# Another order of up and down steps in two Strassen MLPs, and a buffer of its own for one of their weight quads

## The chip, the cores and the metric

The kernel runs on one core of one Trainium2 chip. The metric is the device time of one execution in microseconds, the median of several runs. Before the change it is 1105.84 us (three runs, 1102.9 to 1106.29).

## The reference

A decoder trunk of two layers over 512 tokens of width 1024, in float32. Layer 0 mixes with multi-head latent attention (8 heads, low-rank queries and keys, a rotary part), layer 1 with sliding-window attention (16 query heads over 4 key heads, window 128, a bias by relative position, a sink per head). Each mixer and each MLP is followed by a layer norm of the residual:

```python
# every layer
x = LN(alpha * x + mixer(x))
x = LN(alpha * x + mlp(x))          # alpha = sqrt(2), LN with gain g and bias b

def _mlp(x, w_up, w_down):          # w_up: 1024 x 4096, w_down: 4096 x 1024
    h = jax.nn.relu(x @ w_up)
    return (h * h) @ w_down
```

The output is x after the second layer, 512 x 1024.

## The kernel before, in words

**Arithmetic.** A float32 operand is split into a high part in the matmul format fp32r and a low part, the rest. A product is three matmuls: high by high, high by low, low by high (`three`, `group`; the matmuls are all recorded at L86). A split (L76 to L79) is a copy on ScalarE (ACT, L78) and a subtraction on VectorE (DVE) or GpSimd (POOL), L79. The high part's name ends in h, the low part's in l: `wh`, `wl` are weights, `xth`, `xtl` factors made of x. `fac` holds both parts of a factor of a down step.

**The MLP.** The 4096 hidden columns are four blocks, q = 0 to 3. Each product of a block with x is done by Winograd's form of Strassen's scheme: seven products of half-size matrices in place of eight. So a block has seven up steps, U1 to U7, and, for the first three blocks, seven down steps, D1 to D7; the last block's down product is done plainly, in eight chunks named "down". An up step is 48 matmuls of 256 columns, a down step 24 of 512.

A step multiplies a sum of quarters of x (or of the hidden block) by a sum of quarters of the weights. The hidden block's four quarters are `a11`, `a12`, `a21`, `a22`. They come out of PSUM by sums on DVE as soon as the products they need are done: a12 after U2, a11 after U6, a21 after U7, a22 after U4. Each then goes through a relu and a square on ACT (L622, L623). D1's factor is a11, D2's is a12, and D5, D3, D7, D6 and D4 take sums or single quarters that need a21 and a22.

**Weights.** `queue_seven` makes the sums of weight quarters by memory traffic: quad "a" is loaded by SP for product 1, and after each use a DMA issued by POOL adds another quarter to it in place (L144), for products 5, 6 and 4 in turn. Quad "b" does the same for products 3 and 7; product 2 has a raw tile. Each quad has two halves (jp = 0, 1). The sum for a step can be added only once the split for the step before in that chain has read the quad, and the next split waits until the added quarter has landed. U's quad "b" and D's quad "b" share a tile (`quadb`).

Each step needs two halves of split weights, and there are four buffers for them, so a step's split begins when the step two places back has freed its buffers. A list, `stream`, holds the loads and splits in the order of the steps, and `weights()` keeps it a few entries ahead of the matmuls.

**What sets the order.** Three strings (L41, L42) give the order of steps: `FIRST_STEPS` is the start, `STEPS` the pattern repeated for blocks 0 and 1, `LAST_STEPS` for block 2 with the end; a prime means the next block. TensorE's matmuls are pinned to program order by `pe()`, a call of `keep_in_program_order`. On the other engines a scheduler places the instructions; before the change the loads issued by SP are placed by it too. A dictionary `at` (L668 to L672) says behind which step the code for a down step's factor stands.

**The start of an MLP.** `layer_norm` closes the mixer token tile by token tile, its last operations on POOL (L327, L328), with the gain and bias in a tile `gb` (`load_gb`, L308 and L309). `XFactors.turn` transposes a token tile of x on TensorE (L533), copies it out of PSUM (`xf`, L536), and after the fourth tile makes the sums 5, 3, 6, 7, 4 of x's quarters (L498 to L506) and splits them. Steps U1 and U2 need only the first two tiles; U5 comes next.

**Attention.** The weights of the heads (`w_h`) and of the output projection (`w_o`) are loaded by SP through two `raw` buffers (L115). Beside them SP writes and rereads a table of position biases through DRAM (`ed`, L904, `band`, L907).

Of the kernel before, what the change touches and what calls it, by code (L numbers as in the profile page):

```python
# [8 lines left out]
F32 = mybir.dt.float32  # L9
# [6 lines left out]
P = 128  # L16
D = 1024
# [7 lines left out]
NFF = 4  # L25
# [12 lines left out]

ON_POOL = ("w_h", "w_o", "w_sq", "w_so")

STEPS = "U7 D1 D2 U4 U'1 D5 U'2 D3 U'5 D6 D7 U'3 D4 U'6"  # L41
FIRST_STEPS, LAST_STEPS = "U'1 U'2 U'5 U'3 U'6", "U7 D1 D2 U4 U'1 D5 U'2 D3 U'5 D6 D7 U'3 U'6 U'7 U'4 D4"  # L42

AHEAD_S, AHEAD_B = 3, 2

# [5 lines left out]
def build(tc, nc, io, out):  # L51
    with ExitStack() as top:
# [10 lines left out]
        def nm(s):  # L63
            n_names[0] += 1
            return f"{s}_{n_names[0]}"

        def bank(cols=512, tag="mm", bufs=6):
            return ps.tile([P, cols], F32, tag=tag, bufs=bufs, name=nm(tag), padded_shape=[P, 512])

        def tbank():  # L70
            return bank(512, "tr", 2)

        def f32(ap):
            return ap.bitcast(F32)

        def split(dst_h, dst_l, src, engine=None):  # L76

            nc.scalar.activation(dst_h, src, AF.Copy)  # L78
            (engine or nc.vector).tensor_sub(dst_l, src, f32(dst_h))  # L79

        def pe(ins):
            tc.keep_in_program_order(ins)
# [13 lines left out]
        def tiles_of_weights():  # L96
            wh = wp.tile([P, 1024], F32R, tag="wh", bufs=4, name=nm("wh"))
            wl = wp.tile([P, 1024], F32R, tag="wl", bufs=4, name=nm("wl"))
            return wh, wl

        def raw_tile():
            return wp.tile([P, 1024], F32, tag="raw", bufs=2, name=nm("raw"))

        def queue(name, ap, low=nc.vector):


            def make(pieces=1, between=None):
                cols = ap.shape[-1]
                raw = raw_tile()
                wh, wl = tiles_of_weights()  # L110
                for j in range(pieces):
                    c = slice(j * cols // pieces, (j + 1) * cols // pieces)
                    if between:
                        between(j)
                    nc.sync.dma_start(raw[:, c], ap[:, c])  # L115
                    split(wh[:, c], wl[:, c], raw[:, c], low)
                return wh, wl

            stream.append((name, make))
# [3 lines left out]
        def queue_seven(name, key, chunk):  # L123

            quads = {}

            def half(a, jp):
                if a not in quads:  # L130
                    if (key, a) == ("U", "a"):
                        quads[a] = xp.tile([P, 4, 512], F32, tag="xt", bufs=8, name=nm("wq"))
                    else:
                        quads[a] = mlp_pool[0].tile([P, 4, 512], F32, tag="quad" + a, bufs=1, name=nm("wq"))
                return quads[a][:, 2 * jp : 2 * jp + 2, :]

            def flat(ap):
                return ap.rearrange("p a b -> p (a b)")

            def grown(a, jp, *more):  # L140
                wh, wl = tiles_of_weights()
                split(wh, wl, flat(half(a, jp)))
                if more:
                    nc.gpsimd.dma_start(half(a, jp), chunk(*more, jp), accum_op=ALU.add)  # L144
                return wh, wl

            def loaded(a, jp, at, *more):
                nc.sync.dma_start(half(a, jp), chunk(*at, jp))
                return grown(a, jp, *more)

            def alone(jp):
                raw = raw_tile()
                nc.sync.dma_start(raw.rearrange("p (a b) -> p a b", a=2), chunk(1, 0, jp))
                wh, wl = tiles_of_weights()
                split(wh, wl, raw)
                return wh, wl

            of = {
                1: lambda jp: loaded("a", jp, (0, 0), 0, 1),
                5: lambda jp: grown("a", jp, 1, 1),  # L160
                6: lambda jp: grown("a", jp, 1, 0),
                4: lambda jp: grown("a", jp),
                2: alone,
                3: lambda jp: loaded("b", jp, (1, 1), 0, 1),
                7: lambda jp: grown("b", jp),
            }
# [79 lines left out]
        class Feat:  # L246
# [11 lines left out]
            def turn(self, t):  # L258
                turn_tokens(t, self)
# [4 lines left out]
        b = bank()  # L264
# [28 lines left out]
        half = cp.tile([P, 1], F32, name="half")  # L293
# [10 lines left out]
        xs = [None] * NT  # L304

        def load_gb(g, b):
            gb = xtok.tile([P, 2, D], F32, tag="gb", bufs=1, name=nm("gb"))
            nc.sync.dma_start(gb[:, 0, :], g.partition_broadcast(P))  # L308
            nc.sync.dma_start(gb[:, 1, :], b.partition_broadcast(P))  # L309
            return gb  # L310

        def layer_norm(t, gb, dst):
# [197 lines left out]
        class XFactors(Factors):  # L510
# [14 lines left out]
            def turn(self, t):  # L525
                half_, tk = t // 2, slice(t % 2 * P, (t % 2 + 1) * P)
                if t % 2 == 0:
                    self.xf[half_] = self.mp.tile([P, 2, 4, 256], F32R, tag="fac", bufs=3, name=nm("xf"))
                for n in range(2):
                    pt = tbank().rearrange("p (a b) -> p a b", a=4)  # L530
                    for a in range(4):
                        k = n * 4 + a
                        pe(nc.tensor.transpose(pt[:, a, :], xs[t][:, k * P : (k + 1) * P], ident))  # L533
                    if half_ == 0:
                        split(self.part(n + 1, 0)[:, :, tk], self.part(n + 1, 1)[:, :, tk], pt)
                    nc.scalar.activation(f32(self.xf[half_][:, n, :, tk]), pt, AF.Copy)  # L536
                if t == NT - 1:
                    quarters = [f32(self.xf[i][:, n]) for i in range(2) for n in range(2)]
                    for n in (5, 3, 6, 7, 4):
                        split(self.part(n, 0), self.part(n, 1), self.sum(n, *quarters))  # L540

        def mlp(src, gb, dst, mp):
# [123 lines left out]
            steps = list(steps_of())  # L666

            at = {}  # L668
            for i, (which, q, n) in enumerate(steps):
                if which == "D":  # L670
                    needs = {1: 6, 2: 2, 4: 4}.get(n, 4)
                    i_q = steps.index(("U", q, needs))  # L672
                    i_last = steps.index(("U", q + 1, 6)) - 1 if q == NFF - 2 and n in (4, 7) else i
                    at.setdefault(max(min(i - 2, i_last), i_q), []).append((q, n))
            for i, (which, q, n) in enumerate(steps):
                if which == "U":
# [11 lines left out]
                for q_, n_ in sorted(at.get(i, ()), key=lambda x: [y[2] for y in steps if y[0] == "D" and y[1] == x[0]].index(x[1])):  # L688
                    blocks[q_].factor(n_)

            b = blocks[NFF - 1]
            b.factor(2)
            b.factor(1)
# [19 lines left out]
        with tc.tile_pool(name="mla", bufs=1) as mp:  # L713
# [64 lines left out]
            for kp in range(4):  # L778
                wh, wl = weights("w_kv")
                for t in range(NT):  # L780
                    tk = slice(t * P, (t + 1) * P)
                    for kk in range(2):
                        k, c = 2 * kp + kk, slice(kk * 320, (kk + 1) * 320)
# [19 lines left out]
            for t in range(NT):  # L803
# [194 lines left out]
        xtok = top.enter_context(tc.tile_pool(name="xtok", bufs=1))  # L998

        for t in range(NT):  # L1000
            xs[t] = xtok.tile([P, D], F32, tag="x", bufs=NT, name=nm("x"))
            nc.sync.dma_start(xs[t], io["x"][t * P : (t + 1) * P, :])
        gb = load_gb(io["ln_mix_g"][0], io["ln_mix_b"][0])
        x2 = Feat()
        with tc.tile_pool(name="mlp0", bufs=1) as mp:
            mlp_pool[0] = mp
            x1 = XFactors(mp)
            proj.finish(gb, x1)
            gb = load_gb(io["ln_mlp_g"][0], io["ln_mlp_b"][0])
            mlp(x1, gb, x2, mp)  # L1010


        with tc.tile_pool(name="swa", bufs=1) as mp:
# [56 lines left out]
            pts = [None] * SQH  # L1070
# [103 lines left out]
            run_steps([(h, 0) for h in range(SQH)], AHEAD_B, scores, turn, mix, fill, 1, 1)  # L1174

        gb = load_gb(io["ln_mix_g"][1], io["ln_mix_b"][1])
        with tc.tile_pool(name="mlp1", bufs=1) as mp:
            mlp_pool[0] = mp
            x3 = XFactors(mp)
            proj.finish(gb, x3)  # L1180
            gb = load_gb(io["ln_mlp_g"][1], io["ln_mlp_b"][1])
            mlp(x3, gb, None, mp)


# [107 lines left out]
```

## Time and profile before

| | us |
|---|---|
| median of three runs | 1105.84 |
| profiled execution, its own time | 1104.43 |
| its span, first to last instruction | 1102.7 |
| TensorE (PE) busy in it | 1026.0 (93%) |
| VectorE busy | 785.3 (71%) |
| ScalarE busy | 562.9 (51%) |
| GpSimd busy | 248.6 (23%) |
| mean granted TensorE clock | 0.971 |

The page gives one profiled execution. A row of the timeline has the start, the duration, the engine, the line and the operation with output and inputs; in brackets stands how long the engine was idle before it, and whose result ended that. The waits are the same brackets summed by what ended them: total, times, longest. The granted clock is a share of TensorE's full rate. Up steps begin at 201 us of the span in layer 0 and at 733 us in layer 1.

### The profile page before, as it was taken

How to read it: one execution, taken by the hardware profiler on the slowest of the kernel's cores; microseconds unless marked ns; L12 is line 12 of the kernel's file. 1: busy time of each engine (PE TensorE's matmuls, PEld its weight loads, DVE VectorE, ACT ScalarE, POOL GpSimd, SP SyncE). 2: the span in 40 equal slices, each digit the busy share in tenths (PEclk: the TensorE clock that was granted, in tenths of full speed). 3: DMA queues.
4: the chain of work that ended last, by engine and by line, in shares of the span. 5: the costliest groups of instructions: out<-in, count | busy, mean ns of one | idle time of the engine just before them, and what ended most of it. 6: DMA issues, size and time to landing. Idle time of an engine off the chain costs nothing.

```text
span 1102.7 us, 15934 instructions
## 1 busy us (share of the span) xinstructions
PE 1026.0 (93%) x6148; PEld 909.2 (82%) x6148; DVE 785.3 (71%) x1257; ACT 562.9 (51%) x861; POOL 248.6 (23%) x218
## 2 busy tenths in 40 slices
PE   8999998898998998999999998998899899899996
PEld 7878886797887887888889887887788788788885
DVE  4688855885866856877586788587586686677755
ACT  4456632645634734736156687345473564455530
POOL 0121001511220310320134564043022022112104
PEclk9999998988999998999999999998899999899999
DMA  6241224684884886783242322438568668867432
GB/s 206 89 150 58 91 103 170 129 170 108 180 202 131 176 190 159 150 170 101 85 133 88 96 78 67 147 79 160 143 149 180 175 155 177 203 153 153 81 111 76
DMA packets 60823, 149.55 MB, mean 136 GB/s; under 512 B 5275, under 2 KB 10572, under 8 KB 60748
## 3 DMA queue, kind: packets, MB, share of 16 engines
q0 software_dynamic: 24320, 58.73, 30.3%
q1 hardware_dynamic: 35852, 89.23, 23.7%
q8 instruction: 48, 0.79, 0.3%
q10 hardware_dynamic: 576, 0.59, 0.2%
q14 instruction: 27, 0.22, 0.1%
HBM read 146.41 MB, written 4.22 MB: 137 GB/s over the span
## 4 chain that ended last, share of the span: by engine, by line
PE 48%; issue 19%; DVE 13%; ACT 8%; DMA 7%; POOL 3%; SPq 0%; POOLq 0%; ACTq 0%; DVEq 0%
PE mm L86 43%; DVE wl L79 6%; DMA wq<-in_up 5%; ACT wh L78 4%; PE tr L86 3%; POOL rs L300 1%; ACT a L622 1%; ACT a L623 1%; DVE fac L79 1%; POOL x L328 1%; POOL x L327 1%; DMA xraw<-in_xT 1%; DVE ptl L79 1%; DVE xtl L79 1%; ACT fac L78 1%
## 5 line engine op out<-in xcount | busy, mean ns | idle before, releaser
L86 PE MATMUL mm<-wh,fac 128*128 128x512 f32 (+1 forms) x944 | 305.8, 401 | 28.4 <-ACT fac L78 24.4
L78 ACT ACTIVATE wh<-wq 128x1024 fp32r<-128x1024 f32 x168 | 175.2, 1057 | 247.0 <-DMA wq<-in_up 107.4
L86 PE MATMUL mm<-xth,wh 128*128 128x256 f32 (+1 forms) x1000 | 266.2, 292 | 13.3 <-ACT xth L78 6.1
L79 DVE TENSOR_TENSOR wl<-wq,wh 128x1024 fp32r<-128x1024 f32 x168 | 207.1, 1244 | 90.0 <-ACT wh L78 88.8
L86 PE MATMUL mm<-xth,wl 128*128 128x256 f32 (+1 forms) x872 | 255.2, 293 | 3.0 <-DVE wl L79 3.0
L86 PEld LDWEIGHTS mm<-wh,fac 128*128 128x128 f32 x944 | 181.5, 195 | 74.4 <-ACT fac L78 27.0
L86 PE MATMUL mm<-xtl,wh 128*128 128x256 f32 (+1 forms) x744 | 219.1, 295 | 2.2 <-DVE xtl L79 2.2
L86 PEld LDWEIGHTS mm<-xth,wh 128*128 128x128 f32 x1000 | 184.8, 194 | 18.9 <-ACT xth L78 6.9
L86 PE MATMUL mm<-wl,fac 128*128 128x512 f32 (+1 forms) x472 | 187.8, 398 | 0.0
L86 PEld LDWEIGHTS mm<-xth,wl 128*128 128x128 f32 x872 | 169.0, 194 | 6.3 <-DVE wl L79 4.0
L86 PEld LDWEIGHTS mm<-xtl,wh 128*128 128x128 f32 x744 | 144.5, 194 | 5.5 <-DVE xtl L79 3.0
L78 ACT ACTIVATE wh<-raw 128x1024 fp32r<-128x1024 f32 (+4 forms) x93 | 92.0, 992 | 110.7 <-PE mm L86 58.8
L144 POOL DMA_DIRECT2D wq<-in_up x64 | 77.4, 1211 | 299.6 <-DVE wl L79 290.6
L79 DVE TENSOR_TENSOR wl<-raw,wh 128x1024 fp32r<-128x1024 f32 (+4 forms) x74 | 88.9, 1205 | 50.0 <-ACT wh L78 50.0
L86 PEld LDWEIGHTS mm<-wl,fac 128*128 128x128 f32 x472 | 92.2, 195 | 18.0
L144 POOL DMA_DIRECT2D wq<-in_down x48 | 42.4, 884 | 159.9 <-DVE wl L79 155.9
L300 POOL TENSOR_TENSOR rs<-v,half 128x1 f32<-128x1 f32 x24 | 24.5, 1022 | 238.9 <-DVE v L319 200.9
L79 POOL TENSOR_TENSOR wl<-raw,wh 128x1024 fp32r<-128x1024 f32 (+1 forms) x19 | 40.1, 2115 | 82.9 <-ACT wh L78 78.5
L86 PE MATMUL mm<-wh,oh 128*128 128x512 f32 x128 | 51.9, 405 | 3.0 <-ACT wh L78 3.0
L86 PE MATMUL mm<-wl,oh 128*128 128x512 f32 x128 | 51.0, 399 | 0.5 <-DVE wl L79 0.5
L86 PE MATMUL mm<-wh,ol 128*128 128x512 f32 x128 | 50.9, 398 | 0.0
L454 DVE TENSOR_TENSOR x<-mm,x 128x512 f32<-128x512 f32 (+1 forms) x49 | 32.9, 675 | 21.4 <-PE mm L86 21.0
(196 smaller groups left out, 1795.8 us busy)
## 6 DMA issues: line engine op xcount, KB each, us to landing
wq<-in_up POOLq DMA_DIRECT2D x64, 512.0 KB, 7.8
wq<-in_down POOLq DMA_DIRECT2D x48, 512.0 KB, 8.1
wq<-in_up SPq DMA_DIRECT2D x32, 512.0 KB, 6.1
raw<-in_down SPq DMA_DIRECT2D x28, 512.0 KB, 4.6
wq<-in_down SPq DMA_DIRECT2D x24, 512.0 KB, 6.2
raw<-in_up SPq DMA_DIRECT2D x16, 512.0 KB, 4.7
raw<-in_w_o SPq DMA_DIRECT2D x8, 512.0 KB, 3.3
raw<-in_w_sq SPq DMA_DIRECT2D x8, 512.0 KB, 3.3
```

The source lines that it names most:

```text
L78: nc.scalar.activation(dst_h, src, AF.Copy)
L79: (engine or nc.vector).tensor_sub(dst_l, src, f32(dst_h))
L86: pe(nc.tensor.matmul(dst, st, mv, start=first and i == 0, stop=last and i == len(pairs) - 1, **kw))
L144: nc.gpsimd.dma_start(half(a, jp), chunk(*more, jp), accum_op=ALU.add)
L300: nc.gpsimd.tensor_tensor(r, v, half, ALU.pow)
L327: nc.gpsimd.tensor_mul(x[:, b], x[:, b], gb[:, 0, b])
L328: nc.gpsimd.tensor_add(x[:, b], x[:, b], gb[:, 1, b])
L454: nc.vector.tensor_add(xs[t][:, c], b, xs[t][:, c])
L622: nc.scalar.activation(self.g[done], self.g[done], AF.Relu)
L623: nc.scalar.activation(self.g[done], self.g[done], AF.Square)
```

## The change

Four edits.

1. In the step order, U4 stands behind U7 and ahead of D1 and D2, where it stood behind D2. So U6 and U4 have one step between them in place of three. The rule that places the factors' code is written anew for it.
2. U's quad "b" lies in the tile of the layer norm's gain and bias (`gb`), no longer in the tile that D's quad "b" uses. The norm that follows the MLP therefore loads its gain and bias late, behind the last U7; the load for the norm ahead of the MLP stays where it is, and U's quad "b" follows its last reader.
3. The first sum of x's quarters, for U5, is made per token tile, with the PSUM bank of the transposition as one operand.
4. All loads issued by SP are pinned to program order.

```diff
-STEPS = "U7 D1 D2 U4 U'1 D5 U'2 D3 U'5 D6 D7 U'3 D4 U'6"
-FIRST_STEPS, LAST_STEPS = "U'1 U'2 U'5 U'3 U'6", "U7 D1 D2 U4 U'1 D5 U'2 D3 U'5 D6 D7 U'3 U'6 U'7 U'4 D4"
+STEPS = "U'1 D5 U'2 D3 U'5 D6 D7 U'3 D4 U'6 U'7 U'4 D'1 D'2"
+FIRST_STEPS, LAST_STEPS = "U'1 U'2 U'5 U'3 U'6 U'7 U'4 D'1 D'2", "U'1 D5 U'2 D3 U'5 D6 D7 U'3 U'6 U'7 U'4 D4"
...
-                    nc.sync.dma_start(raw[:, c], ap[:, c])
+                    pe(nc.sync.dma_start(raw[:, c], ap[:, c]))
...
                     if (key, a) == ("U", "a"):
                         quads[a] = xp.tile([P, 4, 512], F32, tag="xt", bufs=8, name=nm("wq"))
+                    elif (key, a) == ("U", "b"):
+                        quads[a] = xtok.tile([P, 4, 512], F32, tag="gb", bufs=1, name=nm("wq"))
...
-                nc.sync.dma_start(half(a, jp), chunk(*at, jp))
+                pe(nc.sync.dma_start(half(a, jp), chunk(*at, jp)))
...
+                pts = []
                 for n in range(2):
                     pt = tbank().rearrange("p (a b) -> p a b", a=4)
+                    pts.append(pt)
...
                     nc.scalar.activation(f32(self.xf[half_][:, n, :, tk]), pt, AF.Copy)
+                if half_ == 1:
+                    if t % 2 == 0:
+                        self.a = self.scratch()
+                    nc.vector.tensor_sub(self.a[:, :, tk], pts[0], f32(self.xf[1][:, 1, :, tk]))
+                    split(self.part(5, 0)[:, :, tk], self.part(5, 1)[:, :, tk], self.a[:, :, tk])
                 if t == NT - 1:
                     quarters = [f32(self.xf[i][:, n]) for i in range(2) for n in range(2)]
-                    for n in (5, 3, 6, 7, 4):
+                    for n in (3, 6, 7, 4):
...
-                    needs = {1: 6, 2: 2, 4: 4}.get(n, 4)
-                    i_q = steps.index(("U", q, needs))
-                    i_last = steps.index(("U", q + 1, 6)) - 1 if q == NFF - 2 and n in (4, 7) else i
+                    i_q = steps.index(("U", q, {1: 6, 2: 2}.get(n, 4)))
+                    i_last = steps.index(("U", q + 1, {2: 2, 3: 2}.get(n, 6))) - 1
                     at.setdefault(max(min(i - 2, i_last), i_q), []).append((q, n))
...
+            gb = gb()
             b = blocks[NFF - 1]
             b.factor(2)
...
-            gb = load_gb(io["ln_mlp_g"][0], io["ln_mlp_b"][0])
-            mlp(x1, gb, x2, mp)
+            mlp(x1, lambda: load_gb(io["ln_mlp_g"][0], io["ln_mlp_b"][0]), x2, mp)
```

The same `pe()` stands around the loads of x, of `gb` and of product 2's raw tile, and the same `lambda` at the second MLP.

**Where instructions move: ScalarE between U6 and D1 of the first block.** The first list is the order before; `wq_409` is U's quad "a", `wq_487` is D's quad "a", the raw tiles are D2's weights, L622 and L623 are the relu and the square, `fac_494` is D1's factor.

```order
L78 ACTIVATE wh_488_2430<-wq_487_2428 128x1024
L78 ACTIVATE wh_495_2499<-wq_487_2428 128x1024
L78 ACTIVATE wh_498_2506<-raw_497_2504 128x1024
L622 ACTIVATE a11_492_2463<-a11_492_2463 128x1024
L78 ACTIVATE wh_505_2570<-raw_504_2568 128x1024
L623 ACTIVATE a11_492_2463<-a11_492_2463 128x1024
L622 ACTIVATE a21_501_2535<-a21_501_2535 128x1024
L78 ACTIVATE fac_494_2495<-a11_492_2463 128x1024
L78 ACTIVATE fac_503_2565<-a12_463_2243 128x1024
L623 ACTIVATE a21_501_2535<-a21_501_2535 128x1024
L78 ACTIVATE wh_507_2574<-wq_409_1910 128x1024
L78 ACTIVATE wh_511_2606<-wq_409_1910 128x1024
```

And the order of the change, where `wq_494` is D's quad "a" and `fac_500` is D1's factor:

```order
L78 ACTIVATE wh_486_2428<-wq_409_1910 128x1024
L78 ACTIVATE wh_492_2492<-wq_409_1910 128x1024
L78 ACTIVATE wh_495_2498<-wq_494_2496 128x1024
L631 ACTIVATE a11_490_2460<-a11_490_2460 128x1024
L78 ACTIVATE wh_501_2562<-wq_494_2496 128x1024
L632 ACTIVATE a11_490_2460<-a11_490_2460 128x1024
L631 ACTIVATE a21_498_2528<-a21_498_2528 128x1024
L78 ACTIVATE fac_500_2558<-a11_490_2460 128x1024
L78 ACTIVATE fac_507_2626<-a12_465_2246 128x1024
L78 ACTIVATE wh_504_2569<-raw_503_2567 128x1024
```

The two copies of U4's weights moved from behind D1's and D2's factors to the place ahead of a11's relu, and D1's and D2's weights each moved one step back; the row of relu, square and factor is as it was. On TensorE U4's 48 matmuls moved ahead of D1's in the same way.

**ScalarE at the start of the MLP.** The order before, from U3's first weight copy on (`wq_460` is U's quad "b", `xth_466` the high part of U5's and U3's factors, `xf` the copied transposes, L605 and L607 the a12 quarter):

```order
L78 ACTIVATE wh_461_2214<-wq_460_2212 128x1024
L605 ACTIVATE a12_463_2243<-mm_452_2141 128x512
L78 ACTIVATE wh_473_2305<-wq_460_2212 128x1024
L605 ACTIVATE a12_463_2243<-mm_454_2168 128x512
L536 ACTIVATE xf_455_2194<-tr_464_2271 128x4x128
L536 ACTIVATE xf_455_2194<-tr_465_2277 128x4x128
L607 ACTIVATE a12_463_2243<-a12_463_2243 128x1024
L78 ACTIVATE xth_466_2283<-uv_468_2285 128x1024
```

The order of the change (`wq_462` is U's quad "b", `xth_458` the factors' high part):

```order
L78 ACTIVATE xth_458_2206<-uv_457_2204 128x4x128
L614 ACTIVATE a12_465_2246<-mm_453_2165 128x512
L540 ACTIVATE xf_454_2191<-tr_466_2274 128x4x128
L616 ACTIVATE a12_465_2246<-a12_465_2246 128x1024
L540 ACTIVATE xf_454_2191<-tr_467_2280 128x4x128
L78 ACTIVATE wh_463_2217<-wq_462_2215 128x1024
L78 ACTIVATE xth_458_2206<-uv_457_2204 128x4x128
L78 ACTIVATE wh_472_2305<-wq_462_2215 128x1024
```

U5's factor is now copied in two halves, the first earlier than its whole was. U3's first weight copy stands between the last `xf` copy and the second half, where it stood ahead of the last tile's copies.

**SP in the attention blocks.** The order before, with the two transfers of the bias table at L904 and L907:

```order
L115 DMA raw_141_715<-in_w_uv 128x1024
L115 DMA raw_159_770<-in_w_h 128x640
L115 DMA raw_186_870<-in_w_h 128x640
L904 DMA ed_148<-p_152_750 16x384
L115 DMA raw_204_955<-in_w_h 128x640
L907 DMA band_149<-ed_148 2048x1x256
L115 DMA raw_241_1112<-in_w_h 128x640
```

And that of the change:

```order
L115 DMA raw_141_715<-in_w_uv 128x1024
L914 DMA ed_148<-p_152_750 16x384
L917 DMA band_149<-ed_148 2048x1x256
L115 DMA raw_159_770<-in_w_h 128x640
L115 DMA raw_186_870<-in_w_h 128x640
L115 DMA raw_204_955<-in_w_h 128x640
L115 DMA raw_241_1112<-in_w_h 128x640
```

Three head-weight loads moved behind the table's two transfers. Further on, the loads of U's quads "a" and "b" and of D's quad "a" for the first block, which stood ahead of the last two `w_o` loads, now stand behind them.

More of the change, by code (lines that the diff above doesn't have):

```diff
@@ L152, in alone @@
                 raw = raw_tile()
-                nc.sync.dma_start(raw.rearrange("p (a b) -> p a b", a=2), chunk(1, 0, jp))
+                pe(nc.sync.dma_start(raw.rearrange("p (a b) -> p a b", a=2), chunk(1, 0, jp)))
                 wh, wl = tiles_of_weights()
@@ L307, in load_gb @@
             gb = xtok.tile([P, 2, D], F32, tag="gb", bufs=1, name=nm("gb"))
-            nc.sync.dma_start(gb[:, 0, :], g.partition_broadcast(P))
-            nc.sync.dma_start(gb[:, 1, :], b.partition_broadcast(P))
+            pe(nc.sync.dma_start(gb[:, 0, :], g.partition_broadcast(P)))
+            pe(nc.sync.dma_start(gb[:, 1, :], b.partition_broadcast(P)))
             return gb
@@ L1001, in build @@
             xs[t] = xtok.tile([P, D], F32, tag="x", bufs=NT, name=nm("x"))
-            nc.sync.dma_start(xs[t], io["x"][t * P : (t + 1) * P, :])
+            pe(nc.sync.dma_start(xs[t], io["x"][t * P : (t + 1) * P, :]))
         gb = load_gb(io["ln_mix_g"][0], io["ln_mix_b"][0])
@@ L1180, in build @@
             proj.finish(gb, x3)
-            gb = load_gb(io["ln_mlp_g"][1], io["ln_mlp_b"][1])
-            mlp(x3, gb, None, mp)
+            mlp(x3, lambda: load_gb(io["ln_mlp_g"][1], io["ln_mlp_b"][1]), None, mp)
 def _const_block():
```

## The prediction

> **What bounds the kernel now.** I read the busy shares first, then TensorE's waits, then the timeline at the longest of them, then the granted clock behind them. The page's first part:
>
> ```profile
> PE 1026.0 (93%) x6148; PEld 909.2 (82%) x6148; DVE 785.3 (71%) x1257; ACT 562.9 (51%) x861; POOL 248.6 (23%) x218
> ```
>
> TensorE is the bound, and the change leaves its matmuls as they are. So only TensorE's idle time and its slow clock can move. Its idle time by what ended it (total, times, longest):
>
> ```profile
> PE mm L86 <- ACT fac L78: 24.4, 9, 3.9
> ...
> PE mm L86 <- ACT wh L78: 4.2, 2, 3.0
> PE mm L86 <- DVE wl L79: 3.8, 7, 0.9
> PE mm L86 <- DVE fac L79: 3.6, 8, 0.5
> PE mm L86 <- DVE uv L612: 3.3, 2, 1.7
> ```
>
> The largest is a wait for a factor ("fac") of a down step. The timeline at its first occurrence, ScalarE (ACT) and VectorE (DVE) rows with the matmul that waits:
>
> ```profile
> 245.79 1.06 ACT L622 ACTIVATE a<-a 128x1024 f32<-128x1024 f32 x1 [0.38 <-DVE a L614]
> ...
> 247.28 1.06 ACT L78 ACTIVATE wh<-raw 128x1024 fp32r<-128x1024 f32 x1 [0.42 <-PE mm L86]
> ...
> 248.24 1.04 ACT L623 ACTIVATE a<-a 128x1024 f32<-128x1024 f32 x1
> ...
> 250.13 1.98 ACT L78 ACTIVATE fac<-a 128x1024 fp32r<-128x1024 f32 x2
> 251.20 2.36 DVE L79 TENSOR_TENSOR fac<-a,fac 128x1024 fp32r<-128x1024 f32 x2 [1.61 <-ACT fac L78]
> ...
> 251.22 0.79 PE L86 MATMUL mm<-wh,fac 128*128 128x512 f32 x1 [3.92 <-ACT fac L78]
> ```
>
> The quarter a11 is complete at 245.8, when U6's last bank has been read. Then ACT does relu, a weight copy that must itself wait for U7 to free a buffer, the square, a relu of a21, and at last D1's factor. U7 is the only step between U6 and D1, and it is over at 247.3. So TensorE stands 3.92 us. The same row comes six times:
>
> ```profile
> 339.29 0.62 PE L86 MATMUL mm<-wh,fac 128*128 128x512 f32 x1 [3.92 <-ACT fac L78]
> 425.39 0.79 PE L86 MATMUL mm<-wh,fac 128*128 128x512 f32 x1 [3.92 <-ACT fac L78]
> 783.56 0.79 PE L86 MATMUL mm<-wh,fac 128*128 128x512 f32 x1 [3.92 <-ACT fac L78]
> 871.74 0.60 PE L86 MATMUL mm<-wh,fac 128*128 128x512 f32 x1 [3.92 <-ACT fac L78]
> 957.53 0.79 PE L86 MATMUL mm<-wh,fac 128*128 128x512 f32 x1 [3.92 <-ACT fac L78]
> ```
>
> What follows the first three, over 8 us (columns: length, TensorE busy, granted clock, DMA share, GB/s; the last row is another gap, below):
>
> ```profile
> 251.20:259.20 8.00, 7.94 (x21) 0.60 0.18 65
> 339.30:347.30 8.00, 7.79 (x27) 0.79 0.17 60
> 425.40:433.40 8.00, 7.96 (x21) 0.61 0.18 65
> 176.60:186.60 10.00, 9.53 (x30) 0.71 0.31 105
> ```
>
> Each gap is paid twice: the wait, and 1.7 to 3.2 us of lost clock behind it (8 us times one minus the clock): 3.2 + 1.7 + 3.1 = 8.0 us for the three of layer 0, 16.0 for the six, with layer 1 taken as layer 0.
>
> **The change part by part.** *U4 ahead of D1 and D2 (six times).* An up step lasts:
>
> ```profile
> 235.79 5.76 PE tr L86 x48
> ...
> 278.76 22.15 PE mm L86 x141
> ```
>
> U4 needs nothing of a11. Put behind U7 it covers 247.3 to 253.1, and D1's factor is there at 251.2 (high part), its low part at 251.20 plus half of 2.36, 252.4. The 3.92 is covered with 0.7 us to spare, and with the gap the cold clock goes: 6 x 3.92 = 23.5, and 16.0. The other factor wait, eight times up to 0.5 (D5's, behind a22), goes too, since a22 comes two down steps earlier: 3.2 for the six in the loops. The third-listed weight wait, up to 0.9, is U3's; its quad now has a buffer of its own and is loaded steps earlier: 2.8 for four of the seven. The two uv waits (3.3), in the last block's U6 to U7, stay. That is 23.5 + 16.0 + 3.2 + 2.8 = 45.5, the lower end.
>
> The other way to count is by periods. The row of 22.15 holds four steps (two up, two down) less 3 of 144 matmuls, so 14 steps take 3.5 x 22.15 x 144/141 = 79.2 us. From D1 to D1 the trace has 88.07 and 86.10 in layer 0 and 88.18 and 85.79 in layer 1. Losses: 8.9 + 6.9 + 9.0 + 6.6 = 31.4, with 7.8 for the first gap of each layer and about 4.6 in each third block (cold 3.2, 0.53, 0.85): 48.4. With a step of 5.76 up and 22.15 / 2 - 5.76 = 5.3 down, the 14 steps would be 77.5, which is 7 more over four periods: 55, the upper end. I take 50.
>
> A rule of the Trainium skill bears on the cold part: "TensorE: Matmul & The Clock Gate", section "What's actually happening", has the clock halved after an idle window of about 3.4 us. The 3.92 gaps agree, but the 2.99 gap at 176.6, with a clock of 0.71 behind it, was shorter than that window. By the rule the clock lost there would not belong to the gap, and the sum below would be 2.9 us smaller; the measurement decides, and I count it.
>
> *The price of that order.* U4's weights come out of quad a, which U6 also used, and an accumulating DMA issued by POOL lies between. U6 and U4 were four steps apart and are now two. That DMA, for U4, alone and among loads at the MLP's start:
>
> ```profile
> L144 POOL DMA_DIRECT2D wq<-in_up x2: 1197/1198/1199, 230.6 to 232.9; - x2
> ...
> DMA to landing us min/median/max: 6.2/6.3/6.4
> ...
> DMA to landing us min/median/max: 10.2/10.7/11.2
> ```
>
> Issued at 230.6, it must be there when ACT copies U4's first half, near 245 (the 1.06 of the copy and 1.23 of the subtraction ahead of 247.3): it may take 14.4 us. At 6.4 there are 8 to spare, at 11.2 still 3. Cost nothing; from below it can gain nothing. What is moved past it: U4 now stands behind U7 on the same bank, whose first half DVE has read 0.7 us after U7's first half, 2 us before U4 writes it.
>
> The Trainium skill, "DMA: Bandwidth & Descriptors", section "Issuing engines are not separate DMA queues", says that POOL's and SP's transfers share the 16 engines; 6.3 alone against 10.7 among loads agrees. That makes the accumulate's landing the number to watch.
>
> *U's quad b in gb's buffer.* U b's load for the first block can now start only when the layer norm has read gb for the last time. At the MLP's start:
>
> ```profile
> 215.37 1.73 POOL L328 TENSOR_TENSOR x<-x,gb 128x320 f32<-128x320 f32 x1
> ...
> 219.62 1.06 ACT L78 ACTIVATE xth<-uv 128x1024 fp32r<-128x1024 f32 x1 [0.35 <-DVE uv L498]
> ...
> 220.73 0.58 PE L86 MATMUL mm<-xth,wh 128*128 128x256 f32 x1 [3.03 <-ACT xth L78]
> 221.99 0.58 PE L86 MATMUL mm<-xtl,wh 128*128 128x256 f32 x1 [0.68 <-DVE xtl L79]
> ```
>
> The load starts at 217.1, and SP's weight loads land after 4.7 to 6.1 us in the median:
>
> ```profile
> wq<-in_up SPq DMA_DIRECT2D x32, 512.0 KB, 6.1
> ...
> raw<-in_up SPq DMA_DIRECT2D x16, 512.0 KB, 4.7
> ```
>
> So it is there near 222. ACT's order now has U3's weight copy between the halves of xth for U5, so ACT stands until 222, then 1.06, half an xth (0.6), and DVE's half subtraction (0.7): 224.4 against 221.99. That eats the gain of making x's sum by tiles, which would have brought xth some 1.5 us forward. Per MLP +2.4 (below: -1.5, if the load is there in time; above: +6, if it lands as the accumulates do, at 10.7); two MLPs: +5.
>
> *Loads in program order, output projection.* One of its weight chunks is late:
>
> ```profile
> 175.50 1.06 ACT L78 ACTIVATE wh<-raw 128x1024 fp32r<-128x1024 f32 x1 [11.66 <-DMA raw<-in_w_o]
> 157.00:177.00 20.00, 17.01 (x76) 13.74 (x74) 8.97 (x13) 4.07 (x5) 0.00 (x0) 0.97 0.86 316
> ...
> 177.87 0.80 PE L86 MATMUL mm<-wl,oh 128*128 128x512 f32 x1 [0.46 <-DVE wl L79]
> ```
>
> SP issued it behind x (2 MB), gb, U's quad b and D's quad a (1 MB each). With its own 0.5 MB that is 5.5 MB, at 316 GB/s 17.4 us from 157, where x is issued. Now only x and gb stand ahead, and U b and D a behind: 2 MB less, 6.3 us earlier, 169. The gap of 2.99, the 0.46 behind it and the cold clock (10 x 0.29 = 2.9) go: -6.4; at worst 0.
>
> *Loads in program order, attention.* SP's rows there:
>
> ```profile
> 71.65 0.64 SPq L907 DMA_DIRECT2D band<-ed  x1
> 75.84 0.33 SPq L115 DMA_DIRECT2D raw<-in_w_h  x1
> ...
> DMA to landing us min/median/max: 11.1/11.1/11.1
> ...
> DMA to landing us min/median/max: 3.1/3.2/7.7
> ```
>
> The band transfer took 11.1 us (the first of the landings), and the weight load of 75.84 landed only at its end (the second is that of the weight loads of this stretch: 7.7 us against 3.2 for its likes). Three w_h loads that stood ahead now stand behind the band, from about 70.5 to 82. ACT's copy for the first of them, which stands behind the first softmax of its head now, waits until 82.3 with the softmax's copies queued behind it, and the next one shifts: PE then stands some 2 + 2 us. I take +4; below 0, since the copies lay off TensorE's path till now, above +10 with a cold clock.
>
> *The rest.* gb for the closing norm is loaded behind U7, and its first use lies behind eight down chunks; four more DVE instructions per MLP lie in 29% of idle DVE time. Nothing; with that cover gone a load of some 6 us, once per MLP.
>
> **Sum.** -50 + 5 - 6.4 + 4 = -47.4. On the span 1102.7 that is 1055.3, on the profiled execution's 1104.43 it is 1057.0; the median of the runs, 1105.84, lies 1.4 above that, so the forecast is 1058.
>
> **The rivals.** *D1 is still late* (0.14). DVE reads the first half of U4's bank ahead of the factor's low part, and ACT has the copies of D1's weights ahead of the factor, as before; only 0.7 us is spare. A wait of 1 to 2.5 us, six times, without the cold clock: 1064 to 1073.
> *The queue in the attention blocks* (0.12): both later copies wait a whole 3.2 load behind the band, and TensorE turns cold: +10 in place of +4, 1064.
> *U4's weights are late* (0.05). If beside other loads the accumulate takes over 14.4 us, each us above is a us of TensorE, six times. At 18 it costs 22, with the cold clock back 38: 1080 to 1096.
> *The same chain, slower than before* (0.05): 47.4 are eaten when 6 x (landing - 14.4) plus 16 of cold clock exceeds them, which is from 19.7 us landing. For it, the accumulate took 10.7 where loads ran beside it, against 6.3 alone, and the new order brings loads closer to it; against it, the chain of waits holds such transfers with no more than this:
>
> ```profile
> 303.28 6.85 DMA wq<-in_up
> ```
> *The change doesn't do what it says* (0.02): were D1 bound by ACT's total work and not by its order, U4's cover would move the wait to D2. ACT is busy 51%, so no.
>
> **How the numbers follow.** The forecast as summed has 0.62. Its own range is 1050 to 1067: 55 in place of 50, or 45.5 and the worst of one of the small terms. With the late D1 and the attention rival (0.26 together) the range reaches to 1078, and 1046 below, where U b's load is in time and the band costs nothing. Faster by over 0.3% (about what a measurement of this kernel can tell from no change) holds the forecast, both small rivals and U4 at under 18 us: 0.94. Slower has the second chain rival: 0.04. Same: 0.02.
>
> **What would show it.** In the profile after: no 3.9 before D1 and a clock of 1.00 in the 8 us behind it; D1 to D1 79 to 81 us; U4's copies with no DMA wait over 1 us; at the MLP's start ACT idle until U3's load lands near 222, and U5's second matmul near 224; no 11.66 before w_o's sixth copy, and its load landing near 169; w_h's fourth copy waiting for DMA until about 82. Wrong it would be if a factor wait of over 1 us stood at D1, or if a wait for the accumulate stood at U4.

## The result, and the profile after

The changed kernel takes 1051.26 us (median of four runs, 1048.46 to 1051.78) against 1104.7 us before (four runs): a ratio of 0.9512, 95% interval 0.9487 to 0.9536. The forecast was 1058 with a range of 1046 to 1078. The profiled execution took 1051.78 us, with a span of 1049.8 us and a mean granted clock of 0.985.

The page's first part, and the largest waits of TensorE (total, times, longest):

```profile
PE 1001.9 (95%) x6148; PEld 898.1 (86%) x6148; DVE 784.8 (75%) x1261; ACT 565.5 (54%) x863; POOL 247.2 (24%) x218
...
PE mm L86 <- ACT xth L78: 13.8, 2, 7.3
PE tr L1131 <- DVE ptl L79: 4.4, 5, 1.4
PE mm L86 <- DVE xtl L79: 2.3, 3, 0.8
PE tr L961 <- DVE pt L79: 2.3, 1, 2.3
```

The wait for ACT's factor, 24.4 us before, is no longer in the list. Nor are the waits for weights of U3 and for uv. In their place stand two long waits for `xth`, at the start of the two MLPs. The matmuls are the same 6148; the busy time fell by 24 us. About 16 of these are clock, by estimate: one minus the mean granted clock, times the span, is 32.0 us before and 15.7 after.

In the loop of an MLP TensorE no longer waits for another engine. The chain of waits of the kernel after (start, length, what, number of instructions), and TensorE in four stretches (length, busy, granted clock, DMA share, GB/s):

```profile
237.87 5.76 PE tr L86 x48
243.63 72.75 PE mm L86 x456
316.38 5.75 PE tr L86 x48
322.13 72.75 PE mm L86 x456
394.88 5.75 PE tr L86 x48
```

```profile
250.00:500.00 250.00, 250.00 (x1597) 1.00 0.82 182
759.00:1000.00 241.00, 241.00 (x1548) 1.00 0.81 183
254.90:262.90 8.00, 8.00 (x38) 1.00 0.69 178
84.90:92.00 7.10, 6.99 (x30) 0.76 0.34 92
```

From U6 to U6 it is 5.75 + 72.75 = 78.5 us with no other engine on the chain, and over 250 us TensorE is busy for all of them at full clock. The third row is D1, which before ran at 0.60 behind a gap of 3.92.

Where the time went, by the start of the same matmul in both traces (columns: length before, length after, difference; the places are named in the prediction):

| stretch | before | after | difference |
|---|---|---|---|
| start to the attention blocks' first transposes (50.35, 51.01) | 50.35 | 51.01 | +0.7 |
| attention, to the wait for `pt` (154.60, 159.24) | 104.25 | 108.23 | +4.0 |
| output projection and norm, to U1's second half (208.68, 208.04) | 54.08 | 48.80 | -5.3 |
| to U5's second matmul, layer 0 (221.99, 223.98) | 13.31 | 15.94 | +2.6 |
| the MLP's loop, layer 0 (575.68, 548.83) | 353.69 | 324.85 | -28.8 |
| layer 1's mixer (741.18, 714.61) | 165.50 | 165.78 | +0.3 |
| to U5's second matmul, layer 1 (754.24, 731.32) | 13.06 | 16.71 | +3.7 |
| the MLP's loop, layer 1, to the end | 348.46 | 318.48 | -30.0 |
| sum | 1102.7 | 1049.8 | -52.9 |

The first stretch lasts 49.4 to 51.8 us and layer 1's mixer 163.7 to 165.9 us in the ten profiled executions of this document, whatever their edits, so the +0.7 and the +0.3 say nothing about the change.

Two places became slower. The start of layer 0's MLP, ScalarE and TensorE:

```profile
215.63 0.55 PE L537 MATMUL tr<-ident,x 128*128 128x128 f32 x3 [0.52 <-POOL x L330]
...
221.01 1.06 ACT L78 ACTIVATE wh<-wq 128x1024 fp32r<-128x1024 f32 x1 [3.68 <-DMA wq<-in_up]
221.97 0.61 ACT L78 ACTIVATE xth<-uv 128x512 fp32r<-128x512 f32 x1
...
222.64 0.58 PE L86 MATMUL mm<-xth,wh 128*128 128x256 f32 x1 [6.46 <-ACT xth L78]
223.98 0.58 PE L86 MATMUL mm<-xtl,wh 128*128 128x256 f32 x1 [0.76 <-DVE xtl L79]
```

ACT stands 3.68 us at U3's weight copy, which nobody needs yet, and the half of `xth` that TensorE waits for is queued behind it. The attention stage:

```profile
83.40 0.74 ACT L78 ACTIVATE wh<-raw 128x640 fp32r<-128x640 f32 x1 [4.22 <-DMA raw<-in_w_h]
...
85.01 0.63 PE L961 MATMUL tr<-ident,p 128*128 128x128 f32 x4 [2.28 <-DVE pt L79]
```

ACT waits 4.22 us for the head weights that SP now issues behind the bias table, TensorE 2.28, and then runs 7 us at a clock of 0.76 (the last of the four rows above), another 1.7 us.

### The profile page after: what moved, and what is told of

It is laid out like the page before. It is cut to its first block, busy times and chain, and to the rows that moved or that the text cites. A ratio compares the mean times of both kernels' runs of the same rounds, so it can differ in the third digit from the quotient of the medians.

```text
span 1049.8 us, 15930 instructions
## 1 busy us (share of the span) xinstructions
PE 1001.9 (95%) x6148; PEld 898.1 (86%) x6148; DVE 784.8 (75%) x1261; ACT 565.5 (54%) x863; POOL 247.2 (24%) x218
## 3 DMA queue, kind: packets, MB, share of 16 engines
HBM read 146.41 MB, written 4.22 MB: 143 GB/s over the span
## 4 chain that ended last, share of the span: by engine, by line
PE 61%; issue 18%; DVE 8%; DMA 6%; POOL 4%; ACT 3%; SPq 0%; POOLq 0%; ACTq 0%; DVEq 0%
PE mm L86 57%; PE tr L86 3%; DVE wl L79 2%; ACT wh L78 1%; POOL rs L302 1%; DMA wq<-in_up 1%; DMA raw<-in_w_h 1%; DVE mm L1103 1%; DVE ptl L79 1%; DMA xraw<-in_xT 1%; POOL x L329 1%; DVE nb L1107 1%; POOL x L330 1%; DMA raw<-in_w_so 1%; ACT p L1111 1%
## 5 line engine op out<-in xcount | busy, mean ns | idle before, releaser
L86 PE MATMUL mm<-wh,fac 128*128 128x512 f32 (+1 forms) x944 | 292.6, 386 | 0.0
L78 ACT ACTIVATE wh<-wq 128x1024 fp32r<-128x1024 f32 x168 | 178.1, 1060 | 210.4 <-PE mm L86 143.4
L86 PEld LDWEIGHTS mm<-wh,fac 128*128 128x128 f32 x944 | 176.3, 188 | 35.5 <-DVE fac L79 0.6
L86 PE MATMUL mm<-wl,fac 128*128 128x512 f32 (+1 forms) x472 | 182.4, 386 | 0.0
L86 PEld LDWEIGHTS mm<-wl,fac 128*128 128x128 f32 x472 | 88.8, 188 | 16.6
```

The lines of the kernel that those rows point to most:

```text
L86: pe(nc.tensor.matmul(dst, st, mv, start=first and i == 0, stop=last and i == len(pairs) - 1, **kw))
```

## The experiments

The theory to be tested: the step order is nearly the whole gain; the other three edits together give little or cost, because each has a gain in one place and a wait in another. Against it stood that the order needs the buffer, and that the buffer carries a large part by itself.

**The order alone.** The kernel before, with the new strings and the new rule for the factors.

```diff
 # before.py
-STEPS = "U7 D1 D2 U4 U'1 D5 U'2 D3 U'5 D6 D7 U'3 D4 U'6"
+STEPS = "U'1 D5 U'2 D3 U'5 D6 D7 U'3 D4 U'6 U'7 U'4 D'1 D'2"
...
-                    i_last = steps.index(("U", q + 1, 6)) - 1 if q == NFF - 2 and n in (4, 7) else i
+                    i_last = steps.index(("U", q + 1, {2: 2, 3: 2}.get(n, 6))) - 1
```

> The kernel before with the new step order and its rule for the factors, and nothing else. Theory A (the order is the change, the rest nearly cancels): the six 3.9 us gaps and the cold clock behind them go, so about -50 against the 1104.7 of before, 1052 to 1058; U3 still waits for its quad b, since D's quad b still shares the tile, and the uv wait of 1.6 to 1.7 us in the last block stays. Theory B (the order needs U's quad b in a buffer of its own, or the accumulating DMA for U4 becomes late): U3's wait grows to 3 us or more each, 1065 to 1085. Theory C (the buffer is not needed at all): every step at its warm length, D1 to D1 78.5 us, 1045 to 1049.

Measured: 1047.31 us, ratio 0.9470 (0.9454 to 0.9485), below the whole change's 1051.26. Theory A's number was too high and the reading of theory C holds, but for one wait. Its waits and a stretch of its loop:

```profile
PE mm L86 <- ACT xth L78: 6.1, 2, 3.0
PE tr L1121 <- DVE ptl L79: 4.5, 5, 1.4
PE mm L86 <- ACT wh L78: 3.9, 2, 3.2
```

```profile
250.00:470.00 220.00, 220.00 (x1407) 1.00 0.83 183
```

The loops take 326.3 and 319.6 us in place of 353.7 and 348.5: 56.3 of the change's 58.8 us. U3's weight waits are gone although U and D share the quad b tile as before. They are gone in the next experiment too, with the old order and a buffer of its own. So those waits took both, the shared tile and the old order. Of the two uv waits 1.6 us are left, 1.27 of them in layer 0's last block.

**Everything but the order.** The changed kernel with the old strings and the old rule.

```diff
 # after.py
-STEPS = "U'1 D5 U'2 D3 U'5 D6 D7 U'3 D4 U'6 U'7 U'4 D'1 D'2"
+STEPS = "U7 D1 D2 U4 U'1 D5 U'2 D3 U'5 D6 D7 U'3 D4 U'6"
...
```

> The changed kernel with the old step order and the old factor rule: buffer, tile sums and loads in program order alone. Theory A: the 3.9 us gaps are back, w_o's gain of 5, attention's loss of 4 and the two late starts of the MLP (2.6 to 3.6 each) nearly cancel against U3's and uv's waits that are gone (some 7 in all): 1098 to 1106, no change that counts. Theory B (the buffer carries a large part of the gain): 1085 or less.

Measured: 1098.12 us, ratio 0.9928 (0.9909 to 0.9948): the low end of theory A's range, and a small gain, not none. The wait for the factor is back:

```profile
PE mm L86 <- ACT fac L78: 25.2, 8, 3.9
```

The loops gain 4.0 and 6.3 us, in layer 0 mostly (3.0) in the last block's U3 to U7, where the weight and uv waits stood; attention and the MLPs' starts come out about as in the changed kernel, and the stretch from w_o to U1 is 1.4 us shorter than there. The two parts do not add: 58.3 for the order alone and 7.5 for the rest would be 65.8, and the whole change gives 53.4. Of the missing 12.4 the loops account for 7.8 (56.3 and 10.3 apart, 58.8 together). What the buffer repairs in the old order the new order has repaired already, so in the new order only its cost at the MLP's start is left, and what the buffer is still worth in a loop, which the fourth experiment measures.

**The old tile for U's quad b.**

```diff
-                    elif (key, a) == ("U", "b"):
-                        quads[a] = xtok.tile([P, 4, 512], F32, tag="gb", bufs=1, name=nm("wq"))
```

> The changed kernel with U's quad b back in the tile it shares with D's quad b. The load for the first block then no longer waits for the layer norm: U5's second matmul of the MLP starts 4 to 5 us earlier than the changed kernel's 223.98, with less cold clock behind it, twice 5 to 7 us; but D's and U's quads again wait for each other: U3 late 0.4 to 0.9 us in each block, uv 1.6 in the last, some 8 in all. Theory A: 1045 to 1052, about as the changed kernel. Theory B (the sharing costs more in the new order): 1060 or more.

Measured: 1045.24 us, ratio 0.9455 (0.9437 to 0.9474). The buffer as the change has it costs about 6 us on balance by the medians, about 4 by the two traces (7.9 at the two starts, from U1's second half to U5's second matmul, less 3.8 in the loops). The waits of U3 in every block that were expected did not come; what came is a wait in each layer's last block (0.63 for uv in layer 1), the first being

```profile
467.52 0.36 PE L86 MATMUL mm<-xth,wh 128*128 128x256 f32 x1 [0.91 <-ACT wh L78]
```

**The buffer for all blocks but the first.** Block 0's quad b lies in the tile shared with D, where nothing is in its way; blocks 1 to 3 keep the `gb` tile. In the edit `first` is true for block 0.

```diff
-                    elif (key, a) == ("U", "b"):
+                    elif (key, a) == ("U", "b") and not first:
                         quads[a] = xtok.tile([P, 4, 512], F32, tag="gb", bufs=1, name=nm("wq"))
```

> The changed kernel, but U's quad b of block 0 alone lies in the tile shared with D's quad b, so that its load need not wait for the layer norm; blocks 1 to 3 keep the buffer. Theory A (ScalarE stands for that load with U5's factor behind it): the xth waits of 6.5 and 7.3 us shrink to about 2, U5's second matmul near 219, with the cold clock behind it less: 1038 to 1043. Theory B (the sums of x bind there whatever the load does): 1049 to 1052.

Measured: 1039.14 us, ratio 0.9400 (0.9384 to 0.9415), as theory A said. U5's start in it:

```profile
216.06 0.38 PE L86 MATMUL mm<-xth,wh 128*128 128x256 f32 x1 [2.40 <-ACT xth L78]
216.79 0.58 PE L86 MATMUL mm<-xtl,wh 128*128 128x256 f32 x1 [0.34 <-DVE xtl L79]
```

2.40 us in place of 6.46, with quad b loaded long before. The two starts are 3.6 and 4.3 us shorter than in the changed kernel. The two profiled spans differ by 13.6; the other 5.7 lie in the kernel's start, attention, the output projection and layer 1's mixer, and the theory does not explain them. The wait itself is: that shows the chain argued for the changed kernel: the norm's last reader of `gb`, the load, U3's weight copy on ACT, and behind it U5's factor. Against the experiment before it, the loops (from U5's first matmul on) are 1.9 and 1.8 us shorter: that is what the buffer is worth in the new order, once its price at the start is not paid.

**The head weights ahead of the bias table.**

```diff
-                    pe(nc.sync.dma_start(raw[:, c], ap[:, c]))
+                    load = nc.sync.dma_start(raw[:, c], ap[:, c])
+                    if name != "w_h":
+                        pe(load)
```

> The changed kernel, with the loads of w_h alone left to the scheduler, so that three of them stand ahead of the bias table's two transfers again, as before the change. Theory (the band's transfer of 11 us holds the loads back, and TensorE waits 2.3 us and then runs at a lower clock): the waits at 83 to 90 us go, about -4: 1046 to 1049. Rival (the attention stage is 4 us longer for another reason, such as ScalarE's order): 1050 to 1052, with the wait for pt still there.

Measured: 1043.62 us, ratio 0.9457 (0.9431 to 0.9483); the median is 2.4 us below the expected range. In its trace the attention stage is 104.25 us long again (from 51.78 to 156.03), 4.0 less than in the changed kernel, and no wait for `pt` or lower clock is there. That stage is settled: the rival is out. The output projection is 1 us shorter as well, but so it is in four runs without this edit (47.4 to 47.8 us against 48.80), and the rest of the difference of the medians is not in one place.

**Both mends together.**

> The changed kernel with both mends: the first block's quad b of U in the tile shared with D, and the loads of w_h left to the scheduler. If the two act in different places they add: 1039.1 less 4, 1034 to 1037. If the earlier loads of w_h collide with something else: 1039 or more.

Measured: 1036.82 us, ratio 0.9390 (0.9366 to 0.9414): faster than the kernel before and than the change, and at the upper end of the range expected if the two add. The intervals of this ratio and of the first mend's overlap, so the times alone do not show that the second mend adds to the first; the trace shows it in its own stage. The attention stage is 104.25 us long again, against 107.44 with the first mend alone, but the median fell by only 2.3 from 1039.14. The profiled execution has layer 1's mixer 2.2 us longer, with the same waits or shorter ones, at a lower clock. The mixer in three stretches, and then the first of them in the run with the first mend alone:

```profile
536.00:600.00 64.00, 61.26 (x407) 0.97 0.21 75
600.00:640.00 40.00, 36.17 (x231) 0.97 0.31 113
640.00:705.00 65.00, 64.25 (x348) 0.97 0.34 97
```

```profile
538.00:602.00 64.00, 61.04 (x412) 1.00 0.23 78
```

Neither mend touches layer 1's mixer. With the same code there the next experiment's run has 165.22 us and a clock of 0.99, so the 2.2 us are a difference between executions, not a price of the mends. What lowers the clock in one execution and not in another is open; the last section has a plainer case.

**The sum of x undone, on top of both mends.**

```diff
-                    nc.vector.tensor_sub(self.a[:, :, tk], pts[0], f32(self.xf[1][:, 1, :, tk]))
-                    split(self.part(5, 0)[:, :, tk], self.part(5, 1)[:, :, tk], self.a[:, :, tk])
...
-                    for n in (3, 6, 7, 4):
+                    for n in (5, 3, 6, 7, 4):
```

> The kernel with both mends, with x's first sum undone: made once from the copied quarters, as before the change. Theory (with quad b out of the way the sum is what U5 waits for): U5's wait goes from 2.4 back to about 3.0, and its second matmul waits 0.7 again, with more cold clock behind: +1.3 to +2.5 for each MLP, 1037 to 1041. Rival (something else binds U5 there): no difference, 1034 to 1037.

Measured: 1040.02 us, ratio 0.9422 (0.9398 to 0.9446). The medians differ by 3.2, and the intervals of the ratios overlap, so the trace decides:

```profile
213.75 0.58 PE L86 MATMUL mm<-xth,wh 128*128 128x256 f32 x1 [3.03 <-ACT xth L78]
215.01 0.58 PE L86 MATMUL mm<-xtl,wh 128*128 128x256 f32 x1 [0.68 <-DVE xtl L79]
```

The wait is back from 2.40 to 3.03, with 0.68 behind it, and the clock from 200 to 250 us is 0.93 in place of 0.97: about 2 us more at that one place (50 x 0.04), besides the waits. The sum by tiles is a gain, which in the changed kernel was hidden under the longer wait for quad b.

**How late may the accumulate for U4 be?** The changed kernel, with that one addition to quad a issued twice; U4's weights are then not the right sum.

```diff
-                    nc.gpsimd.dma_start(half(a, jp), chunk(*more, jp), accum_op=ALU.add)
+                    for _ in range(2 if key == "U" and more == (1, 0) else 1):
+                        nc.gpsimd.dma_start(half(a, jp), chunk(*more, jp), accum_op=ALU.add)
```

> The changed kernel, in which POOL adds the last quarter of U's quad a (for U4) twice, one after the other, so U4's weights are not the right sum: this measures how much later the accumulate may land. By the working of the prediction (8 us to spare for the first half, some 6 for the second): the two halves' four transfers in a row would put the second half some 2 to 4 us too late, 6 times: 1058 to 1076, with a wait for the weights at U4. If the spare is much smaller than worked out: over 1085. If it is larger, or the transfers overlap: 1050 to 1054.

Measured: 1098.77 us, ratio 0.9958 (0.9941 to 0.9975): far over the expected 1058 to 1076. Nearly the whole gain of the change is gone by one transfer more per half. Its largest wait, and the second block in its trace (ACT, DVE, then TensorE):

```profile
PE mm L86 <- DVE a L627: 33.6, 8, 5.3
```

```profile
325.61 1.06 ACT L78 ACTIVATE wh<-wq 128x1024 fp32r<-128x1024 f32 x1 [8.16 <-DMA wq<-in_up]
...
329.21 2.00 ACT L78 ACTIVATE wh<-wq 128x1024 fp32r<-128x1024 f32 x2 [2.55 <-DMA wq<-in_up]
...
331.44 0.68 DVE L624 TENSOR_TENSOR a<-mm,uv 128x512 f32<-128x512 f32 x1
332.04 0.68 DVE L627 TENSOR_TENSOR a<-uv,mm 128x512 f32<-128x512 f32 x1
...
332.87 0.77 PE L86 MATMUL mm<-xth,wh 128*128 128x256 f32 x2 [5.01 <-DVE a L627]
```

The wait comes at all eight U4 steps, 1.8 and 2.6 us in each layer's first block and 4.4 to 5.3 in the others, and it has another name than expected. It isn't U4's weights that TensorE lacks, it is U7's bank: the low part of U4's weights stands on DVE ahead of the subtraction that reads U7's product (L627), and U4 writes the same bank. DVE, held by the late weights, holds the reading back. And it comes earlier than the weights would be missed. In the changed kernel the second half's transfer, issued at 313.44, is there at 322.52, 9.1 us later, and ACT waits for it:

```profile
322.52 1.06 ACT L78 ACTIVATE wh<-wq 128x1024 fp32r<-128x1024 f32 x1 [1.45 <-DMA wq<-in_up]
```

With two transfers (the first issued at 313.42) it is there at 329.21, 15.8 us later. 6.7 us more delay made a gap of 5.0: the changed kernel has 1.7 us to spare in this block, and the landing may take some 10.8 us, not 14.4. The changed kernel's own rows give the same: DVE has read the bank at 326.03, the end of this row, and U4's first matmul starts at 327.73.

```profile
325.35 0.68 DVE L626 TENSOR_TENSOR a<-uv,mm 128x512 f32<-128x512 f32 x1
```

## Why the prediction was right, and where it was off

**The order.** Right in its mechanism and its place, and undersized: the loops gained 58.8 us, where 50 was taken and 55 was the upper end. Two terms were too small. The step that set a warm block of 14 steps to 79.2 us (3.5 x 22.15 x 144/141) was too high; it measures 78.5, which makes the losses of the four periods 34.1 in place of 31.4. And "about 4.6 in each third block" measures 7.6 in layer 0: 3.3 for D1 and D2 at the lower clock, 0.4 at U4 and U'1, 0.9 at D5, and 3.1 in U'3 to U'4 (each from the steps' starts in the two traces). The listed gap of a wait can be less than what the step loses: U'3 to U'4 had 0.85 + 1.71 in brackets and lost 3.1.

**"The two uv waits stay."** Wrong. The order alone leaves 1.6 of the 3.3 us, everything but the order leaves none. In the new order a wait is there without the buffer (0.91 for weights in layer 0's last block and 0.63 for uv in layer 1's, in the third experiment) and gone with it in blocks 1 to 3 (the fourth). So the buffer removes them, and the step that gave them a place in the last block and left them there failed. How U3's quad makes uv late was not tried by itself, but the trace before shows a chain. ACT stands 7.45 us for the load of U3's quad b, then 4.18 and 2.83 for the two halves that POOL adds to it for U7; the low part of the second half stands on DVE ahead of the additions to uv, and TensorE waits for these:

```profile
483.42 1.06 ACT L78 ACTIVATE wh<-wq 128x1024 fp32r<-128x1024 f32 x1 [7.45 <-DMA wq<-in_up]
496.44 1.06 ACT L78 ACTIVATE wh<-wq 128x1024 fp32r<-128x1024 f32 x1 [2.83 <-DMA wq<-in_up]
497.53 1.23 DVE L79 TENSOR_TENSOR wl<-wq,wh 128x1024 fp32r<-128x1024 f32 x1 [2.66 <-ACT wh L78]
499.39 0.69 DVE L612 TENSOR_TENSOR uv<-mm,uv 128x512 f32<-128x512 f32 x1
500.23 0.36 PE L86 MATMUL mm<-xth,wh 128*128 128x256 f32 x1 [1.71 <-DVE uv L612]
```

It is the chain of the last experiment: late weights hold DVE, and DVE holds TensorE.

**U's quad b in gb's buffer.** Right in place, size and chain: +2.4 was predicted, U5's second matmul near 224.4; it was 223.98, +2.6, and in layer 1 +3.7, where the load took 6.2 us and not the 5.4 of layer 0. The longer gaps of 6.5 and 7.3 us cost no more clock behind them than the 3.03 before: over the 15 us from U5's first matmul on it is 0.78 and 0.86, against 0.80 and 0.79. The fourth experiment shows the cause.

**The output projection.** -6.4 predicted, -5.3 measured. The wait of 2.99 is gone, and the cold clock behind it too (1.00 over the 10 us from 174.24 on). The load's landing had moved less far than worked out:

```profile
175.80 1.06 ACT L78 ACTIVATE wh<-raw 128x1024 fp32r<-128x1024 f32 x1 [7.32 <-DMA raw<-in_w_o]
```

The stage itself starts 4.6 us later than before (159.24 against 154.60), behind the longer attention, so the 169 of the prediction, 14.4 us after the start, became 173.6; it landed 16.6 after it, and a wait of 0.61 for the low part is left at 180.50. In four other runs with the same loads (the second, third, fourth and last experiment) the landing comes 15.3 to 16.0 us after the start, that wait is gone, and the stretch gains 6.3 to 6.7. So the term was right, and the missing 1.1 us are this execution's.

**Attention.** +4 predicted, +4.0 measured; one wait of 2.28 in place of two of about 2, and 1.7 of lower clock that had been put into the upper bound. That the number agrees to a tenth is luck. In the four other runs with the same loads there are two waits, of 1.6 to 2.2 and of 1.1 to 1.2, at full clock, and the stage is 3.2 to 3.8 us longer than before: the two waits of the prediction, the second smaller than taken. The fifth experiment shows the cause.

**The accumulate.** Of the signs that the prediction named, this one is not met: ACT waits 1.45 us for U4's weights, where no wait over 1 us was to be seen, though TensorE does not wait. "At 6.4 there are 8 to spare, at 11.2 still 3": wrong, though the forecast did not suffer. In the loop the landing takes 9.1, not the 6.4 that was read from the first block, and only 1.7 us are to spare. The error was to count the time until the weights are used, and not that DVE, which makes their low part, has in its order to read the bank that U4 writes. So the rival on the other side of zero stood nearer than its 19.7 us: at 15.8 only 5 of the 53 us were left.

**The sum.** -58.8 + 6.3 - 5.3 + 4.0 + 1.0 (start and layer 1's mixer) = -52.8, against -47.4: the loops 8.8 better than taken, the other places together 3.4 worse. The two misses cancel in part, so the total was nearer than its largest term.

## What to carry to other kernels

When an engine waits for a chain of small operations, look for a whole step that is ready and move it into the gap; here that single reordering gave 58 us, and the edits around it cost 4 on balance. Edits that each remove a wait need not add: ask whether the first has removed the cause of the second, and test each alone against the kernel before. When a load is moved, look at what stands behind its consumer on that engine: a copy that nobody needs yet, placed ahead of one that the bottleneck needs, costs as much as the load is late.

## What the runs showed that was not expected

The same wait lowers the clock in one execution and not in another. In layer 1's mixer TensorE waits 1.82 us for ACT, at the same matmul, in all ten profiled executions. Over the 5 us behind it the clock is 0.66 in five of them (the changed kernel and the second, third, fifth and seventh experiment) and 1.00 in the other five. The changed kernel, then the run with the first mend alone:

```profile
597.16 0.50 PE L86 MATMUL mm<-xth,wh 128*128 128x512 f32 x1 [1.82 <-ACT p L1111]
597.16:602.16 5.00, 5.00 (x17) 0.66 0.41 143
...
589.13 0.50 PE L86 MATMUL mm<-xth,wh 128*128 128x512 f32 x1 [1.82 <-ACT p L1111]
589.13:594.13 5.00, 5.00 (x30) 1.00 0.42 140
```

In the attention stage the changed kernel's wait of 2.28 us, with another of 1.04 some 4 us ahead of it, was followed by 7 us at 0.76. The second experiment waits 2.16 us at that place, also behind one of 1.04, and keeps a clock of 1.00 over the next 7 us, and so does the first mend with 1.63:

```profile
82.92 0.63 PE L961 MATMUL tr<-ident,p 128*128 128x128 f32 x4 [1.63 <-DVE pt L79]
...
70.00:110.00 40.00, 35.86 (x200) 1.00 0.36 112
```

So these runs show no length of a gap from which on the clock falls; what else decides it is open. One such place makes two executions of the same code differ by 1.7 us (5 x 0.34). The Trainium skill, "TensorE: Matmul & The Clock Gate", section "What's actually happening", has an idle window of about 3.4 us; the waits here are shorter, and the measurement decides.

A wait on a PSUM bank can be the first sign of a late load: in the last experiment the row names a subtraction on DVE, and the transfer that caused it appears only in ACT's own rows, 4 to 7 us earlier.
